# A trunk kernel on one Trainium2 core: six attention heads of layer 1 multiply whole fp32 values in four-pass products, two heads to a PSUM bank

## The chip, the core and the metric

The kernel runs on one core of a Trainium2 chip. The core has five engines that work side by side: PE (TensorE, the matrix engine; its weight loads are shown as PEld), DVE (VectorE), ACT (ScalarE), POOL (GpSimd) and SP (SyncE, which issues the DMAs here). PE writes its results to PSUM, eight banks of 128 rows by 512 fp32 columns; POOL works on SBUF alone in this kernel. The metric is the device time of one execution in microseconds (us); less is better.

## The reference, cut to what matters

Two decoder layers on 512 tokens of width 1024, all in fp32. Layer 0 has a sparse attention of another kind, layer 1 has the "NSA" mixer; each runs beside a small attention over 256 memory rows, and each layer ends in a SwiGLU block. The change concerns layer 1's 12 token heads of 64 columns each, in two groups of six that share keys and values. Head by head, three softmax results are multiplied with three sets of values and summed with gates:

```python
    o_c = jnp.einsum('btgjc,bcgd->btgjd', p_c.astype(v_cmp.dtype), v_cmp)
    ...
    o_s = jnp.einsum('bgtjk,bgtkd->btgjd', p_s, v_sel)
    ...
    o_w = jnp.einsum('btgjk,bkgd->btgjd', p_w, vw_i)
    o = gi[..., 0:1] * o_c + gi[..., 1:2] * o_s + gi[..., 2:3] * o_w
```

`o_c` is the compressed branch (31 compressed keys), `o_s` the selected-block branch and `o_w` the window branch. With 512 tokens both of these see every earlier key.

## The kernel before, in words

Everything is kept transposed, with channels on the partitions and the 512 tokens on the columns. To keep fp32 precision on PE, most operands are split into two fp32r parts, hi (the value rounded to fp32r) and lo (what is left), and a product is made of two or three fp32r matmuls (`mm3`, lines 177 to 179). Where an operand stays plain fp32, one matmul instruction does a full-precision product; the change calls this "four-pass".

Layer 1 is a written-out order of units (`SEQ[1]`, line 51): `q:j` projects the queries of head pair j, `h:n` and `w:n` make the softmax rows of head n for the selected and the window branch (`nsa_first`), `H:n` and `W:n` multiply them with the values (`nsa_second`), `c:j` and `C:j` are the compressed branch of a pair, `m`, `o` and others belong to the memory heads and the output projection. Tile, the framework, turns this order into one fixed queue per engine, by its own simulated times, and adds the semaphores.

A unit `H:n` or `W:n` treats its four key blocks in three groups (`KBS`, line 43), of 512, 128 + 384 and 256 columns. For each group it

- transposes the softmax blocks on PE into a "T" bank (line 418, ten transposes of 128x128 to a unit),
- copies the bank to `uh` on ACT (line 426), rounded to fp32r, and subtracts it from the bank on DVE to give `ul` (line 427),
- multiplies each block with the values (line 441), once for `uh` and once for `ul`. The stationary operand is 128 columns wide: 64 of the hi part of the values beside 64 of their lo part.

So the head's "O" bank holds the products with the hi values on rows 0 to 63 and those with the lo values on rows 64 to 127. The compressed branch adds one more fp32r matmul of 512 columns to each head (line 1041), whose operand `ch` is again a hi part on 64 rows (ACT, line 1025) and a lo part on the other 64 (DVE, line 1026). Then `head_out` folds the two halves: an ACT copy of one half (line 449), a DVE add of the other (line 450), the hi part on ACT (line 150) and the lo part on DVE or POOL (line 452 or 83).

The tables in `PLAN` say which engine does which small step; layer 1 runs on rows 4, 5 and then 6, and its turned blocks all take the `"turn": "V"` of row 5, the path just described. Another path, `"F"` (lines 420 to 423), stands in layer 0: one ACT copy to a plain fp32 tile `uf` and one plain fp32 matmul with the 128-column values.

The "O" tag has two banks, "T" four, "S" and "mm" two each; projections take "mm" and "O" in turn.

Of the kernel before, what the change touches and what calls it, by code (L numbers as in the profile page):

```python
# [18 lines left out]
P = 128  # L19
S = 512  # L20
D = 1024
KC = D // P
NB = S // P
NM = 256
# [5 lines left out]
OUT = -3e38  # L30
DOWN_SPLIT = (6, 5)
HALVED = 2
LAST = ("PPVP", "VVVV")
BUFS = {"xs": 17, "p": 10, "u": 8, "q": 12, "z": 2, "q1": 8, "qi": 4, "cy": 2, "k": 8, "m": 6, "r": 3, "t": 6, "o": 26, "o2": 6, "xg": 8}
RINGS = {"wr": 4, "wh": 3, "wl": 3}
STAY = {F32: 7 * KC + 2 + P + KC * S + S + P + NM + 1024 + 592 + RINGS["wr"] * KC * P, F32R: 4 * NB * P + 6 * P + (RINGS["wh"] + RINGS["wl"]) * KC * P}
BANKS = {"mm": 2, "S": 2, "T": 4, "O": 2}
FIRST = (0, 3)
IQ = False
# [3 lines left out]
KBS = ((0,), (3, 1), (2,))  # L43
# [8 lines left out]
 w:5 W:3 C:2 h:4 c:3 q:5 h:5 H:5 mq:0 c:4 H:4 h:6 W:4 C:3 W:5 H:6 c:5 h:8 h:9 mq:1 h:7 mkv w:6 w:7 H:7 m:0 W:6 W:7 o:5 H:8 C:4 w:9 M:0 o:3  # L52
 o:2 m:1 o:1 h:10 o:0 H:9 o:6 W:9 w:8 w:10 M:1 o:7 o:4 W:8 C:5 h:11 H:10 o:12 o:11 w:11 H:11 W:10 o:13 W:11 o:9 o:14 o:8 o:10 o:15"""]
PLAN = [
    {"w": "V", "whi": "A", "stack": "P", "turn": "VP", "scale": "V", "shi": "A", "hhi": "VA", "hlo": "VP", "rmul": "VV", "radd": "V", "phi": "V", "plo": "V", "sqe": "PP", "irow": "VVPP", "sq": "PV"},
    {"w": "PP", "whi": "A", "stack": "P", "turn": "VFF", "scale": "P", "shi": "A", "hhi": "AA", "hlo": "PP", "rmul": "P", "radd": "PV", "phi": "VAAV", "plo": "PPP", "sqe": "AAP", "irow": "P", "sq": "VPP"},
    {"w": "P", "whi": "A", "stack": "VP", "turn": "V", "scale": "PAVA", "shi": "VVV", "hhi": "A", "hlo": "PV", "rmul": "VPVP", "radd": "PV", "phi": "VVV", "plo": "P", "sqe": "PP", "irow": "VPV", "sq": "VP"},
    {"w": "PPV", "whi": "AA", "stack": "PV", "turn": "F", "scale": "PP", "shi": "V", "hhi": "VVVV", "hlo": "VV", "rmul": "P", "radd": "PPP", "phi": "VVV", "plo": "V", "sqe": "VAPV", "irow": "P", "sq": "P"},
    {"w": "VVP", "whi": "VA", "stack": "PV", "turn": "FF", "scale": "A", "shi": "AVA", "hhi": "AA", "hlo": "PV", "rmul": "VV", "radd": "VPV", "phi": "AVVV", "plo": "VPVP", "sqe": "VA", "irow": "VVVV", "sq": "V"},
    {"w": "P", "whi": "AA", "stack": "P", "turn": "V", "scale": "VV", "shi": "A", "hhi": "A", "hlo": "VPP", "rmul": "PVV", "radd": "PP", "phi": "A", "plo": "PV", "sqe": "PA", "irow": "P", "sq": "VPPV"},  # L60
    {"w": "PPP", "whi": "A", "stack": "P", "turn": "V", "scale": "A", "shi": "V", "hhi": "A", "hlo": "VV", "rmul": "PPP", "radd": "P", "phi": "VV", "plo": "V", "sqe": "AVP", "irow": "PVVV", "sq": "PP"},
]
SWAP = [i ^ 8 if i < 16 else i for i in range(32)]
W0 = ["kk", "qi0", "qi1", "qi2", "qi3", "ckv", "qm0", "qm1"] + [f"q{j}" for j in range(6)]
# [3 lines left out]
def r32(ap):  # L68
    return ap.bitcast(F32)
# [25 lines left out]
class Trunk:  # L95
# [543 lines left out]
    def down_last(self, acts):  # L639

        nc, cs, ws = self.nc, range(KC - HALVED, KC), []
        for c in cs:
# [14 lines left out]
        for h in range(2):  # L657
# [294 lines left out]
    def comp_values(self, hv, cw2):  # L952
        nc = self.nc
        ps = self.ps("S")[:, :P]
        for g in range(2):
            nc.tensor.matmul(ps[:64, g * 64 : (g + 1) * 64], hv[:, g], cw2[:, P:], start=True, stop=True)
        self.vc = vc = self.c([P, 2, 2, P], F32R, name="vcmp")
        nc.gpsimd.memset(r32(vc), 0.0)
        src = ps.rearrange("p (g d) -> p g d", g=2)
        for par in range(2):  # L960
            h = slice(32 * par, 32 * par + 32)
            a, b = slice(0, 64), slice(64, P)
            nc.scalar.activation(vc[h, :, par, a], src[h], AF.Copy, scale=0.5)
            for up in (0, 64):
                hu = slice(32 * par + up, 32 * par + up + 32)
                if up:
                    nc.scalar.copy(vc[hu, :, par, a], r32(vc[h, :, par, a]))
                nc.vector.scalar_tensor_tensor(vc[hu, :, par, b], src[h], 0.5, r32(vc[h, :, par, a]), op0=ALU.mult, op1=ALU.subtract)

    def values(self, col, xs):  # L970

        nc, io = self.nc, self.io
        gates = self.gates
        self.ready.add("values")
        ncol = self.small(NB, "ncol", bufs=1)
        nc.vector.tensor_scalar(ncol, col, -1.0, None, op0=ALU.mult)
        out = [self.ps(t)[:, :292] for t in ("mm", "O", "mm", "O")]
        for u in range(3):
            ks = range(3 * u, min(3 * u + 3, KC))
            wt = self.weight(io["w1v"][:, ks.start * 292 : ks.stop * 292], len(ks) * 292)  # L980
            for b in range(NB):
                for i, k in enumerate(ks):
                    self.mm3(out[b], tuple(t[:, b * P : (b + 1) * P] for t in xs[k]), tuple(t[:, i * 292 : (i + 1) * 292] for t in wt),
                             k == 0, k == KC - 1)
        for b in range(NB):
            src = out[b][:, :256].rearrange("p (a d) -> p a d", a=4)
            v = self.vals[:, :, b]
            s = col[:, b : b + 1]
            nc.scalar.activation(v[:, :, 0:64], src, AF.Copy, scale=s)
            nc.vector.scalar_tensor_tensor(v[:, :, 64:128], src, s, r32(v[:, :, 0:64]), op0=ALU.mult, op1=ALU.subtract)  # L990
            nc.scalar.activation(gates[:, b], out[b][:, 256:292], AF.Exp, scale=ncol[:, b : b + 1])
        nc.vector.tensor_scalar(gates, gates, 1.0, None, op0=ALU.add)

# [25 lines left out]
    def compressed_turned(self, j, p):  # L1019
        nc = self.nc  # L1020
        ps = self.ps("T")
        for b in range(NB):
            nc.tensor.transpose(ps[:64, b * P : (b + 1) * P], p[:, b * 64 : (b + 1) * 64], self.ident)
        c = self.slot("t", "ch", F32R)
        nc.scalar.copy(c[:64], ps[:64])
        nc.vector.tensor_sub(c[64:], ps[:64], r32(c[:64]))
        self.comp[j] = c

    def nsa_units(self, h, q, keys):
        j, e, g = h // 2, h % 2, h // 6  # L1030
        shared = {}

        def first(br):
            return self.nsa_first(h, q[h], keys[br][g], br)

        def second(br, ps_):
            if br == 0:
                shared["o"] = self.ps("O")
            self.nsa_second(h, br, shared["o"], ps_)
            if br == 1:  # L1040
                self.nc.tensor.matmul(shared["o"], self.vc[:, g, e], self.comp[j], start=False, stop=True)
                hs = slice(64 * e, 64 * e + 64)
                self.head_out(shared["o"], slice(0, S), e, self.o[j][0][hs], self.o[j][1][hs])
                self.whole[j] += 1

        return [(lambda: first(0), lambda st: second(0, st)), (lambda: first(1), lambda st: second(1, st))]

    def comp_unit(self, j):
        return lambda: self.compressed(j), lambda st: self.compressed_turned(j, st)
# [17 lines left out]
    def nsa_second(self, h, br, o, ps_):  # L1067
        nc = self.nc
        e, g = h % 2, h // 6
        for kbs in KBS:  # L1070
            at, pieces, spans = 0, [], []
            for kb in kbs:
                pieces += [(at + (b - kb) * P, ps_[b][:, kb * P : (kb + 1) * P]) for b in range(kb, NB)]
                spans.append((kb, slice(at, at + S - kb * P)))
                at += S - kb * P
            parts = self.turned(pieces, at)
            for kb, cs in spans:
                self.weighted(o[:, kb * P :], self.vals[:, 2 * br + g, kb], [t[:, cs] for t in parts], br == 0 and kb == 0, False)

    def run(self):  # L1080
        self.turn, self.flip, self.comp, self.two, self.ready = False, False, {}, {}, set()
# [86 lines left out]
```

## Time and profile before

| | |
|---|---|
| time, median of 3 runs | 1277.14 us (1274.31 to 1278.22) |
| the profiled execution | 1273.98 us |
| its span, first to last instruction | 1272.2 us |
| mean granted PE clock | 0.990 |
| instructions | 17057 |
| PE busy | 1226.5 us (96%) |
| DVE busy | 631.0 us (50%) |
| ACT busy | 546.5 us (43%) |
| POOL busy | 769.0 us (60%) |

The profiled execution is a run of its own, with 1.8 us outside the span. Its busy times are averages over stages: the FFN blocks (about 200 to 640 us and from 890 us on) keep PE full, the two attention stages less so. A PE instruction's recorded duration includes a tail during which the next one already runs, so what a matmul costs is read from the distance between two starts.

### The profile page before, as it was taken

Reading aid. Unit: us, or ns where it says so; the run is one execution under the profiler, and the core shown is the slowest. Engines: PE = TensorE matmul, PEld = TensorE weight load, DVE = VectorE, ACT = ScalarE, POOL = GpSimd, SP = SyncE. Lnnn points to the kernel's source line nnn. Section 1 sums busy time; section 2 is a strip of 40 time slices with the busy share of each in tenths; the row PEclk is TensorE's granted clock in tenths of the full one; section 3 lists DMA queues with packets and bytes.
Section 4 is the critical chain, followed back from the end, with each engine's and each line's share of the span. In section 5 each row is a group of like instructions: output and inputs, shape, how many; then the busy total and the mean of one; then the engine's idle time right before and its main releaser. Section 6 shows DMA issues by size and latency. Waiting matters only on the chain. (4 is left out here: it accounts for less than half of the span.)

```text
span 1272.2 us, 17057 instructions
## 1 busy us (share of the span) xinstructions
PE 1226.5 (96%) x5882; PEld 1016.1 (80%) x5882; DVE 631.0 (50%) x1433; ACT 546.5 (43%) x1059; POOL 769.0 (60%) x1070
## 2 busy tenths in 40 slices
PE   7999889999999999999997899999999999999996
PEld 5888558888888888888886788887888888888886
DVE  7799976632221222233678998996531210111113
ACT  5635886332322222322257677785432322332231
POOL 9988874855543455447276553235977656667573
PEclk9999999999999999999998999999999999999998
DMA  7222002233323332223332001113233233333232
GB/s 272 85 86 80 9 1 92 85 98 99 90 81 102 121 90 97 89 82 121 103 100 66 24 13 45 44 32 111 84 102 95 83 91 116 107 97 92 69 91 67
DMA packets 40262, 108.44 MB, mean 85 GB/s; under 512 B 4720, under 2 KB 10480, under 8 KB 40176
## 3 DMA queue, kind: packets, MB, share of 16 engines
q1 hardware_dynamic: 40176, 107.36, 27.5%
q8 instruction: 46, 0.75, 0.3%
q14 instruction: 40, 0.33, 0.1%
HBM read 105.25 MB, written 2.10 MB: 84 GB/s over the span
## 5 line engine op out<-in xcount | busy, mean ns | idle before, releaser
L83 POOL TENSOR_TENSOR stay<-stay,stay 128x256 fp32r<-128x256 f32 (+1 forms) x601 | 442.3, 765 | 323.3 <-ACT stay L150 181.5
L150 ACT CAST stay<-stay 128x1024 fp32r<-128x1024 f32 (+4 forms) x208 | 189.4, 911 | 511.8 <-PE ps L178 452.0
L177 PE MATMUL ps<-xh,stay 128*128 128x512 f32 x912 | 357.6, 392 | 7.8 <-ACT xh L238 6.2
L179 PE MATMUL ps<-xh,stay 128*128 128x512 f32 x912 | 358.1, 393 | 1.2 <-DVE stay L165 1.1
L178 PE MATMUL ps<-xl,stay 128*128 128x512 f32 x912 | 357.5, 392 | 0.9 <-DVE xl L239 0.9
L177 PEld LDWEIGHTS ps<-xh,stay 128*128 128x128 f32 x912 | 172.6, 189 | 44.2 <-ACT xh L238 6.2
L179 PEld LDWEIGHTS ps<-xh,stay 128*128 128x128 f32 x912 | 172.5, 189 | 37.9 <-DVE stay L165 2.0
L178 PEld LDWEIGHTS ps<-xl,stay 128*128 128x128 f32 x912 | 172.2, 189 | 37.5 <-DVE xl L239 2.1
L178 PE MATMUL ps<-fl,stay 128*128 128x512 f32 (+1 forms) x352 | 134.8, 383 | 0.0
L179 PE MATMUL ps<-fh,stay 128*128 128x512 f32 (+1 forms) x352 | 134.6, 382 | 0.0
L177 PE MATMUL ps<-fh,stay 128*128 128x512 f32 (+1 forms) x352 | 134.6, 382 | 0.0
L609 DVE TENSOR_TENSOR fa<-fa,ps 128x512 f32<-128x512 f32 x44 | 30.2, 687 | 183.5 <-PE ps L179 166.1
L626 DVE TENSOR_TENSOR stay<-stay,ps 128x512 f32<-128x512 f32 x30 | 20.7, 689 | 155.5 <-PE ps L179 155.5
L606 DVE TENSOR_TENSOR fa<-ps,row 128x512 f32<-128x512 f32 x44 | 30.2, 691 | 129.5 <-PE ps L179 116.2
L391 ACT ACTIVATE p<-p,stay 128x384 f32<-128x384 f32 (+3 forms) x144 | 80.3, 559 | 22.9 <-DVE stay L385 21.3
L83 POOL TENSOR_TENSOR fa<-fa,row 128x256 f32<-128x256 f32 x88 | 65.3, 763 | 25.3 <-ACT fa L607 25.2
L178 PEld LDWEIGHTS ps<-fl,stay 128*128 128x128 f32 x352 | 66.1, 188 | 12.9
L179 PEld LDWEIGHTS ps<-fh,stay 128*128 128x128 f32 x352 | 66.1, 188 | 12.9
L177 PEld LDWEIGHTS ps<-fh,stay 128*128 128x128 f32 x352 | 66.1, 188 | 12.9
L427 DVE TENSOR_TENSOR ul<-ps,uh 128x512 fp32r<-128x512 f32 (+1 forms) x103 | 62.1, 619 | 5.4 <-ACT uh L426 4.7
L426 ACT CAST uh<-ps 128x512 fp32r<-128x512 f32 (+1 forms) x103 | 53.3, 533 | 12.5 <-PE ps L418 11.6
L418 PE MATMUL ps<-stay,p 128*128 128x128 f32 x360 | 54.3, 275 | 4.5 <-DVE stay L385 1.6
(273 smaller groups left out, 1981.2 us busy)
## 6 DMA issues: line engine op xcount, KB each, us to landing
stay<-in_wf SPq DMA_DIRECT2D x88, 512.0 KB, 3.6
stay<-in_w SPq DMA_DIRECT2D x26, 512.0 KB, 3.6
stay<-in_wd SPq DMA_DIRECT2D x32, 384.0 KB, 3.1
stay<-in_wd SPq DMA_DIRECT2D x32, 320.0 KB, 2.8
mem<-in_memT SPq DMA_DIRECT2D x12, 256.0 KB, 3.9
stay<-in_wo SPq DMA_DIRECT2D x6, 512.0 KB, 3.6
stay<-in_wo SPq DMA_DIRECT2D x16, 192.0 KB, 2.4
stay<-in_xT SPq DMA_DIRECT2D x8, 256.0 KB, 6.8
```

Source lines behind the costliest of these rows:

```text
L83: op(out[:, sl], x[:, sl], y[:, sl])
L150: self.nc.scalar.copy(out, x)
L177: mm(out, lhs[0], rhs[0], start=start, stop=False)
L178: mm(out, lhs[0], rhs[1], start=False, stop=False)
L179: mm(out, lhs[1], rhs[0], start=False, stop=stop)
L391: self.nc.scalar.activation(p, p, AF.Exp, scale=-1.0, bias=least, accum_out=total)
L418: nc.tensor.transpose(ps[:, off : off + P], ap, self.ident)
L426: nc.scalar.copy(hi, ps[:, :w])
L427: nc.vector.tensor_sub(lo, ps[:, :w], r32(hi))
L606: nc.vector.tensor_mul(a, g, row)
L609: nc.vector.tensor_mul(a, a, u)
L626: nc.vector.tensor_add(self.x[d], self.x[d], ps)
```

## The change

For the heads of group 0 (heads 0 to 5, `WHOLE = (0,)`) the values are no longer split. Heads 6 to 11 stay as they are.

- `values` writes the group's values to a plain fp32 tile with one ACT instruction for each token block, and the split (ACT, then DVE) is made for the other group alone. `comp_values` likewise makes the compressed values of group 0 as one plain tile for the two heads of a pair.
- `whole_second` takes the place of `nsa_second`: the same transposes, one ACT copy of the bank to a plain tile `uf`, and one four-pass matmul for each block with 64 stationary columns, whose result goes to rows 0 to 63 of a bank for the even head and to rows 64 to 127 of the same bank for the odd head. The `ul` subtraction is gone.
- `compressed_turned` keeps a plain copy on 64 rows for these pairs; one four-pass matmul of 512 columns serves both heads of the pair.
- `head_out` is not called for these heads. When both branches of both heads are in the bank, `hi` is copied from it on ACT and `lo` is subtracted from it on DVE, 128 rows at once.

The diff, cut to its core:

```diff
+WHOLE = (0,)
...
 PLAN = [
...
+    {"w": "P", "full": "A", "whi": "A", "stack": "P", "turn": "V", "scale": "VV", "shi": "A", "hhi": "A", "hlo": "VPP", "rmul": "PVV", "radd": "PP", "phi": "A", "plo": "PV", "sqe": "PA", "irow": "P", "sq": "VPPV"},
...
     def comp_values(self, hv, cw2):
...
+            if g in WHOLE:
+                self.vc[g] = vc = self.c([P, P], name="vcmp")
+                nc.gpsimd.memset(vc, 0.0)
+                for par in range(2):
+                    h = slice(32 * par, 32 * par + 32)
+                    nc.scalar.activation(vc[h, 64 * par : 64 * par + 64], src[h], AF.Copy, scale=0.5)
+                continue
...
     def values(self, col, xs):
...
+        self.whole_vals = {g: self.c([P, 2, NB, 64], name="wv") for g in WHOLE}
...
+            for g in range(2):
+                if g in WHOLE:
+                    nc.scalar.activation(self.whole_vals[g][:, :, b], src[:, g::2], AF.Copy, scale=s)
+                    continue
+                v = self.vals[:, g::2, b]
+                nc.scalar.activation(v[:, :, 0:64], src[:, g::2], AF.Copy, scale=s)
+                nc.vector.scalar_tensor_tensor(v[:, :, 64:128], src[:, g::2], s, r32(v[:, :, 0:64]), op0=ALU.mult, op1=ALU.subtract)
...
-        c = self.slot("t", "ch", F32R)
-        nc.scalar.copy(c[:64], ps[:64])
-        nc.vector.tensor_sub(c[64:], ps[:64], r32(c[:64]))
+        if j // 3 in WHOLE:
+            c = self.slot("t", "ch")
+            nc.scalar.copy(c[:64], ps[:64])
...
         def second(br, ps_):
+            if g in WHOLE:
+                return self.whole_second(h, br, ps_)
...
+    def whole_second(self, h, br, ps_):
+        nc = self.nc
+        j, e, g = h // 2, h % 2, h // 6
+        if j not in self.pairs:
+            self.pairs[j] = [self.ps("O"), set()]
+        o, done = self.pairs[j]
+        rows = slice(64 * e, 64 * e + 64)
+        for kbs in KBS:
+            pieces, spans, at = self.gathered(kbs, ps_)
+            ps = self.ps("T")
+            for off, ap in pieces:
+                nc.tensor.transpose(ps[:, off : off + P], ap, self.ident)
+            t = self.slot("u", "uf")[:, :at]
+            self.copy("full", t, ps[:, :at])
+            for kb, cs in spans:
+                nc.tensor.matmul(o[rows, kb * P :], self.whole_vals[g][:, br, kb], t[:, cs], start=kb == 0 and not any(d[0] == e for d in done),
+                                 stop=False, skip_group_check=True)
+        done.add((e, br))
+        if len(done) == 4:
+            nc.tensor.matmul(o, self.vc[g][:64], self.comp[j][:64], start=False, stop=True, skip_group_check=True)
+            hi, lo = self.o[j]
+            self.copy("hhi", hi, o)
+            nc.vector.tensor_sub(lo, o, r32(hi))
+            self.whole[j] += 2
```

`gathered` is the loop of `nsa_second` that collects the blocks of a group, moved to a function of its own.

## Rows read from the trace of the kernel before

**Rows 1.** The page, part 1: busy time, share of the span and instructions of each engine.

```profile
PE 1226.5 (96%) x5882; PEld 1016.1 (80%) x5882; DVE 631.0 (50%) x1433; ACT 546.5 (43%) x1059; POOL 769.0 (60%) x1070
```

**Rows 2.** Busy time of each engine in stretches of layer 1's attention stage: the stretch, its length, then busy us and instructions of PE, PEld, DVE, ACT and POOL, the granted PE clock, DMA share, GB/s.

```profile
660.00:690.00 30.00, 24.58 (x139) 20.86 (x138) 25.90 (x74) 22.62 (x58) 22.17 (x30) 0.89 0.23 71
690.00:776.00 86.00, 79.07 (x483) 67.73 (x482) 84.00 (x248) 61.49 (x157) 41.58 (x56) 1.00 0.07 20
776.00:890.00 114.00, 110.80 (x606) 94.56 (x606) 96.96 (x258) 79.52 (x208) 41.06 (x62) 1.00 0.22 63
```

**Rows 3.** Who PE's matmuls waited for between 690 and 776 us: total us, times, longest us.

```profile
PE ps L441 <- DVE ul L427: 3.7, 4, 1.7
PE ps L418 <- DVE stay L385: 1.6, 2, 1.3
PE ps L380 <- DVE rb L329: 0.7, 1, 0.7
PE ps L177 <- DVE ul L427: 0.7, 1, 0.7
```

**Rows 4.** The same waits seen from PE's weight loads, between 690 and 776 us.

```profile
PEld ps L441 <- DVE ul L427: 5.8, 8, 2.1
PEld ps L418 <- DVE stay L385: 2.1, 2, 1.5
PEld ps L177 <- DVE ul L427: 1.1, 1, 1.1
PEld ps L380 <- DVE rb L329: 0.9, 1, 0.9
PEld ps L380 <- DVE stay L385: 0.7, 2, 0.4
```

**Rows 5.** Groups of DVE's instructions between 690 and 776 us: line, shapes, count, busy us, mean ns of one, idle time before.

```profile
L427 DVE TENSOR_TENSOR ul<-ps,uh 128x512 fp32r<-128x512 f32 x24 | 16.1, 680 | 0.0
L427 DVE TENSOR_TENSOR ul<-ps,uh 128x256 fp32r<-128x256 f32 x12 | 4.9, 406 | 0.1
L450 DVE TENSOR_TENSOR ho<-ho,ps 64x512 f32<-64x512 f32 x6 | 4.0, 674 | 0.1
```

**Rows 6.** Two more of DVE's lines between 690 and 776 us, each from the view of its own line or tile: count, duration in ns (least, median, most), first and last start.

```profile
L452 DVE TENSOR_TENSOR ol<-ho,oh x2: 689/954/1220, 712.0 to 752.2; 64x512 fp32r<-64x512 f32 x2
L1026 DVE TENSOR_TENSOR ch<-ps,ch x4: 684/684/685, 697.4 to 771.5; 64x512 fp32r<-64x512 f32 x4
```

**Rows 7.** Groups of ACT's instructions between 690 and 776 us, as in rows 5.

```profile
L426 ACT CAST uh<-ps 128x512 fp32r<-128x512 f32 x24 | 13.6, 577 | 4.4 <-PE ps L418 4.1
L449 ACT COPY ho<-ps 64x512 f32<-64x512 f32 x6 | 3.5, 581 | 2.6 <-PE ps L1041 2.5
```

**Rows 8.** The timeline of PE's matmuls from 706 us on: start, recorded duration, line, shapes, count, and in brackets the idle time before it and what ended it.

```profile
706.21 0.33 PE L441 MATMUL ps<-ul,stay 128*128 128x128 f32 x1 [1.68 <-DVE ul L427]
706.37 0.39 PE L441 MATMUL ps<-uh,stay 128*128 128x384 f32 x1
706.60 0.34 PE L441 MATMUL ps<-ul,stay 128*128 128x384 f32 x1
706.78 0.28 PE L441 MATMUL ps<-uh,stay 128*128 128x256 f32 x1
706.90 0.27 PE L418 MATMUL ps<-stay,p 128*128 128x128 f32 x1
```

**Rows 9.** The timeline of PE's matmuls in layer 0, where plain fp32 products (`uf`, and `mem` in the second part) stand among fp32r ones.

```profile
128.96 0.39 PE L441 MATMUL ps<-ul,stay 128*128 128x512 f32 x1
129.19 1.02 PE L441 MATMUL ps<-uf,stay 128*128 128x512 f32 x2
129.64 0.80 PE L177 MATMUL ps<-mkh,oh 128*128 128x512 f32 x1
130.28 0.40 PE L178 MATMUL ps<-mkl,oh 128*128 128x512 f32 x1
...
111.51 2.97 PE L489 MATMUL ps<-mem,stay 128*128 128x256 f32 x13
114.32 0.38 PE L505 MATMUL ps<-stay,mem 128*128 128x256 f32 x1
```

**Rows 10.** The timeline of PE's matmuls around four instructions whose stationary operand has 64 columns (128*64).

```profile
693.77 0.28 PE L381 MATMUL ps<-tl,sa 128*128 128x256 f32 x1
693.89 0.60 PE L1023 MATMUL ps<-stay,pc 128*64 128x128 f32 x4
694.33 0.49 PE L418 MATMUL ps<-stay,p 128*128 128x128 f32 x3
```

**Rows 11.** Layer 0's plain copies of a turned bank, from the view of line 422 (count, duration in ns as least, median and most, first and last start), and, from the view of line 441, the idle time that PE and PEld had before that line until such a copy came (us, times).

```profile
L422 ACT COPY uf<-ps x15: 560/585/605, 127.0 to 178.4; 128x512 f32<-128x512 f32 x15
...
  ACT uf L422: 3.1, 5
```

**Rows 12.** The timeline of PE's matmuls, one line of head 0's first unit.

```profile
676.80 0.48 PE L441 MATMUL ps<-ul,stay 128*128 128x128 f32 x1 [0.76 <-DVE ul L427]
```

**Rows 13.** Who PE's weight loads waited for between 776 and 890 us, two of the rows.

```profile
PEld ps L177 <- DVE stay L385: 1.5, 1, 1.5
PEld ps L441 <- DVE ul L427: 1.4, 3, 0.8
```

More of the change, by code (lines that the diff above doesn't have):

```diff
@@ L35 @@
 RINGS = {"wr": 4, "wh": 3, "wl": 3}
-STAY = {F32: 7 * KC + 2 + P + KC * S + S + P + NM + 1024 + 592 + RINGS["wr"] * KC * P, F32R: 4 * NB * P + 6 * P + (RINGS["wh"] + RINGS["wl"]) * KC * P}
+STAY = {F32: 7 * KC + 2 + P + KC * S + S + P + NM + 1024 + 592 + len(WHOLE) * (2 * NB * 64 + P) + RINGS["wr"] * KC * P, F32R: 4 * NB * P + 6 * P + (RINGS["wh"] + RINGS["wl"]) * KC * P}
 BANKS = {"mm": 2, "S": 2, "T": 4, "O": 2}
@@ L54 @@
 PLAN = [
-    {"w": "V", "whi": "A", "stack": "P", "turn": "VP", "scale": "V", "shi": "A", "hhi": "VA", "hlo": "VP", "rmul": "VV", "radd": "V", "phi": "V", "plo": "V", "sqe": "PP", "irow": "VVPP", "sq": "PV"},
-    {"w": "PP", "whi": "A", "stack": "P", "turn": "VFF", "scale": "P", "shi": "A", "hhi": "AA", "hlo": "PP", "rmul": "P", "radd": "PV", "phi": "VAAV", "plo": "PPP", "sqe": "AAP", "irow": "P", "sq": "VPP"},
-    {"w": "P", "whi": "A", "stack": "VP", "turn": "V", "scale": "PAVA", "shi": "VVV", "hhi": "A", "hlo": "PV", "rmul": "VPVP", "radd": "PV", "phi": "VVV", "plo": "P", "sqe": "PP", "irow": "VPV", "sq": "VP"},
@@ L58 @@
-    {"w": "PPV", "whi": "AA", "stack": "PV", "turn": "F", "scale": "PP", "shi": "V", "hhi": "VVVV", "hlo": "VV", "rmul": "P", "radd": "PPP", "phi": "VVV", "plo": "V", "sqe": "VAPV", "irow": "P", "sq": "P"},
-    {"w": "VVP", "whi": "VA", "stack": "PV", "turn": "FF", "scale": "A", "shi": "AVA", "hhi": "AA", "hlo": "PV", "rmul": "VV", "radd": "VPV", "phi": "AVVV", "plo": "VPVP", "sqe": "VA", "irow": "VVVV", "sq": "V"},
-    {"w": "P", "whi": "AA", "stack": "P", "turn": "V", "scale": "VV", "shi": "A", "hhi": "A", "hlo": "VPP", "rmul": "PVV", "radd": "PP", "phi": "A", "plo": "PV", "sqe": "PA", "irow": "P", "sq": "VPPV"},
@@ L61 @@
-    {"w": "PPP", "whi": "A", "stack": "P", "turn": "V", "scale": "A", "shi": "V", "hhi": "A", "hlo": "VV", "rmul": "PPP", "radd": "P", "phi": "VV", "plo": "V", "sqe": "AVP", "irow": "PVVV", "sq": "PP"},
+    {"w": "V", "full": "A", "whi": "A", "stack": "P", "turn": "VP", "scale": "V", "shi": "A", "hhi": "VA", "hlo": "VP", "rmul": "VV", "radd": "V", "phi": "V", "plo": "V", "sqe": "PP", "irow": "VVPP", "sq": "PV"},
+    {"w": "PP", "full": "A", "whi": "A", "stack": "P", "turn": "VFF", "scale": "P", "shi": "A", "hhi": "AA", "hlo": "PP", "rmul": "P", "radd": "PV", "phi": "VAAV", "plo": "PPP", "sqe": "AAP", "irow": "P", "sq": "VPP"},
@@ new lines @@
+    {"w": "P", "full": "A", "whi": "A", "stack": "VP", "turn": "V", "scale": "PAVA", "shi": "VVV", "hhi": "A", "hlo": "PV", "rmul": "VPVP", "radd": "PV", "phi": "VVV", "plo": "P", "sqe": "PP", "irow": "VPV", "sq": "VP"},
+    {"w": "PPV", "full": "A", "whi": "AA", "stack": "PV", "turn": "F", "scale": "PP", "shi": "V", "hhi": "VVVV", "hlo": "VV", "rmul": "P", "radd": "PPP", "phi": "VVV", "plo": "V", "sqe": "VAPV", "irow": "P", "sq": "P"},
+    {"w": "VVP", "full": "A", "whi": "VA", "stack": "PV", "turn": "FF", "scale": "A", "shi": "AVA", "hhi": "AA", "hlo": "PV", "rmul": "VV", "radd": "VPV", "phi": "AVVV", "plo": "VPVP", "sqe": "VA", "irow": "VVVV", "sq": "V"},
@@ L62 @@
+    {"w": "P", "full": "A", "whi": "AA", "stack": "P", "turn": "V", "scale": "VV", "shi": "A", "hhi": "A", "hlo": "VPP", "rmul": "PVV", "radd": "PP", "phi": "A", "plo": "PV", "sqe": "PA", "irow": "P", "sq": "VPPV"},
+    {"w": "PPP", "full": "A", "whi": "A", "stack": "P", "turn": "V", "scale": "A", "shi": "V", "hhi": "A", "hlo": "VV", "rmul": "PPP", "radd": "P", "phi": "VV", "plo": "V", "sqe": "AVP", "irow": "PVVV", "sq": "PP"},
 ]
@@ L956, in comp_values @@
             nc.tensor.matmul(ps[:64, g * 64 : (g + 1) * 64], hv[:, g], cw2[:, P:], start=True, stop=True)
[L957 to L968, printed above, removed]
+        self.vc = {}
+        for g in range(2):
+            src = ps[:, g * 64 : (g + 1) * 64]
+            if g in WHOLE:
[5 more added lines that the diff above has]
+                continue
+            self.vc[g] = vc = self.c([P, 2, P], F32R, name="vcmp")
+            nc.gpsimd.memset(r32(vc), 0.0)
+            for par in range(2):
+                h = slice(32 * par, 32 * par + 32)
+                a, b = slice(0, 64), slice(64, P)
+                nc.scalar.activation(vc[h, par, a], src[h], AF.Copy, scale=0.5)
+                for up in (0, 64):
+                    hu = slice(32 * par + up, 32 * par + up + 32)
+                    if up:
+                        nc.scalar.copy(vc[hu, par, a], r32(vc[h, par, a]))
+                    nc.vector.scalar_tensor_tensor(vc[hu, par, b], src[h], 0.5, r32(vc[h, par, a]), op0=ALU.mult, op1=ALU.subtract)
     def values(self, col, xs):
@@ L986, in values @@
             src = out[b][:, :256].rearrange("p (a d) -> p a d", a=4)
-            v = self.vals[:, :, b]
             s = col[:, b : b + 1]
-            nc.scalar.activation(v[:, :, 0:64], src, AF.Copy, scale=s)
-            nc.vector.scalar_tensor_tensor(v[:, :, 64:128], src, s, r32(v[:, :, 0:64]), op0=ALU.mult, op1=ALU.subtract)
+            for g in range(2):
+                if g in WHOLE:
[4 more added lines that the diff above has]
+                nc.vector.scalar_tensor_tensor(v[:, :, 64:128], src[:, g::2], s, r32(v[:, :, 0:64]), op0=ALU.mult, op1=ALU.subtract)
             nc.scalar.activation(gates[:, b], out[b][:, 256:292], AF.Exp, scale=ncol[:, b : b + 1])
@@ L1023, in compressed_turned @@
             nc.tensor.transpose(ps[:64, b * P : (b + 1) * P], p[:, b * 64 : (b + 1) * 64], self.ident)
-        c = self.slot("t", "ch", F32R)
-        nc.scalar.copy(c[:64], ps[:64])
-        nc.vector.tensor_sub(c[64:], ps[:64], r32(c[:64]))
+        if j // 3 in WHOLE:
+            c = self.slot("t", "ch")
+            nc.scalar.copy(c[:64], ps[:64])
+        else:
+            c = self.slot("t", "ch", F32R)
+            nc.scalar.copy(c[:64], ps[:64])
+            nc.vector.tensor_sub(c[64:], ps[:64], r32(c[:64]))
         self.comp[j] = c
@@ L1040, in second @@
             if br == 1:
-                self.nc.tensor.matmul(shared["o"], self.vc[:, g, e], self.comp[j], start=False, stop=True)
+                self.nc.tensor.matmul(shared["o"], self.vc[g][:, e], self.comp[j], start=False, stop=True)
                 hs = slice(64 * e, 64 * e + 64)
@@ L1070, in nsa_second @@
         for kbs in KBS:
[L1071 to L1075, printed above, removed]
+            pieces, spans, at = self.gathered(kbs, ps_)
             parts = self.turned(pieces, at)
@@ L1078, in nsa_second, with gathered @@
                 self.weighted(o[:, kb * P :], self.vals[:, 2 * br + g, kb], [t[:, cs] for t in parts], br == 0 and kb == 0, False)
+    def gathered(self, kbs, ps_):
+        at, pieces, spans = 0, [], []
+        for kb in kbs:
+            pieces += [(at + (b - kb) * P, ps_[b][:, kb * P : (kb + 1) * P]) for b in range(kb, NB)]
+            spans.append((kb, slice(at, at + S - kb * P)))
+            at += S - kb * P
+        return pieces, spans, at
     def run(self):
+        self.pairs = {}
         self.turn, self.flip, self.comp, self.two, self.ready = False, False, {}, {}, set()
```

## The prediction

> **What bounds the kernel now.** The page first: PE is busy 96% of the span [rows 1], so one would look for a gain in PE's own work. That share is an average. The stretches of layer 1's attention show another stage [rows 2]: from 690 to 776 us, which holds the products of heads 0 to 5 except the first unit of head 0, DVE is busy 84.00 of 86 us while PE shows 79.07. From 776 to 890 us, where heads 6 to 11 run, DVE falls to 96.96 of 114. So in the first stretch DVE is full and PE waits for it; behind it PE is the bound again.
>
> The waits say the same. Between 690 and 776 us all that the matmuls waited for is DVE [rows 3]: 3.7 + 0.7 us for `ul`, 1.6 us for a score read out late (line 385), 0.7 us for a rope step. The weight loads show longer waits for the same things, 5.8 + 1.1 us and 2.1 + 0.9 + 0.7 us [rows 4]. The two views bracket the truth. A 512-column fp32r matmul is recorded with 0.39 us, while the next starts 0.23 us later [rows 9], so each matmul wait is shown about 0.16 us too short, and waits under 0.16 us are not shown. A weight load runs ahead of its matmul, so its wait is shown too long.
>
> **What the change takes from DVE.** The twelve units of heads 0 to 5 have 24 subtractions of 512 columns and 12 of 256, as many as the stretch shows: 24 x 0.680 + 12 x 0.406 = 21.2 us [rows 5]. (The stretch misses head 0's first unit and holds one of head 6.) The six adds of `head_out` go, 6 x 0.674 = 4.0 us [rows 5], two `lo` subtractions, 2 x 0.954 = 1.9 us, and three of `ch`, 3 x 0.684 = 2.1 us [rows 6]. What comes is three `lo` subtractions from PSUM at 128x512, by the same shape's 0.680 us: 2.0 us. Together 27.2 us less, nearly a third of DVE's 84.00 us.
>
> That is off PE's own queue, so only the waits turn into time.
>
> - Waits for `ul`: 4.4 us in five waits [rows 3], with 0.16 us added to each 5.2 us, and a little for four short ones that only the weight loads show [rows 4]. I take 5.5; the bounds are 4.4 and 6.9.
> - Waits for scores and rope, 2.3 us in three waits [rows 3], with the tails 2.8; bounds 0 and 3.7 [rows 4]. These steps stand in DVE's queue behind the subtractions that go, but each also has work of its own ahead of it. I take two thirds, 1.9 us.
> - Head 0's first unit, before the stretch, waited 0.76 us for `ul` [rows 12], with the tail 0.9 us. What is late next after it is its last blocks' copy on ACT, idle a quarter of that stretch [rows 2], so I take all of it.
>
> **What it changes on PE.** The transposes stay. A unit's eight fp32r matmuls become four plain ones. Their step is in layer 0: from the first `uf` product (129.19) to the second fp32r matmul behind the pair (130.28) is 1.09 us, less 0.23 for the fp32r one 0.86, so 0.43 us for each 512 columns; thirteen of 256 columns take 2.81 us, 0.216 each [rows 9]. That is 0.84 ns a column, and 1280 columns of a unit cost 1.08 us. The fp32r unit costs 2 x 0.23 for 512 columns, 0.23 + 0.18 for 384, 0.12 twice for 256 [rows 8, 9], and for the two of 128 columns 0.06 each by columns: 1.23 us. So 0.15 us a unit, 1.8 us in twelve; by columns alone (0.23 / 512) it would be 1.15 us a unit and 0.9 us in all. The three pairs' compressed products change 2 x 0.23 into 0.43, 0.1 us. I take 1.5; the bounds are 0.9 and 1.9.
>
> No row has a plain product of 64 columns that lands on rows 64 to 127. The nearest are the compressed branch's transposes, 128*64 on rows 0 to 63: the first follows the 256-column matmul before it by 0.12 us, its usual step, four of them take 0.44 us, as do the 128*128 ones behind them by their starts (0.11 each), and neither switch shows a gap [rows 10]. I take nothing for switching and 0.84 ns a column for 64 columns too. The upper bound is a drained array at each switch (below).
>
> The Trainium skill speaks against this: "TensorEngine Tiling (Array Packing)", Key Properties, says that a change of tiling mode, though not of the tile, drains the engine. The trace does not agree for its one pair of switches, 0.12 and 0.11 us by the steps in [rows 10]; by the rule the sum would shrink by 72 drains. Its page "FP8 and Floating Point Precision", TensorE Precision Notes, says a true fp32 product takes four passes; if a pass cost what an fp32r matmul costs, 512 columns would be 0.92 us by an estimate, where [rows 9] give 0.43.
>
> **What it adds on ACT.** The copy to `uf` takes the place of the one to `uh`, 0.585 us against 0.577 [rows 7, 11]. Six copies of 0.581 us [rows 7] and six `hi` copies leave for three `hi` copies of 128x512. `values` gains four ACT instructions of half the width. All of it is hidden: ACT has 61.49 us of work in the 86 [rows 2]; without that cover, each would cost its own 0.3 to 0.6 us. But now PE waits for ACT where it waited for DVE. Layer 0's fifteen such copies made PE and its loads wait 3.1 us in all [rows 11], 0.2 us each, which for 36 copies would be 7.4 us. In the stretch itself 36 copies on the same queue caused no wait that [rows 3] list. I take a cost of 1.0 us, near the row from the stage itself.
>
> A pair now holds one "O" bank from its first product to its last copies, where each head held one in turn. A projection or the next pair queues for the other bank. I take nothing: two heads in succession held as long, and overlapping heads held two.
>
> **The sum.** 5.5 + 1.9 + 0.9 + 1.5 - 1.0 = 8.8 us. The profiled execution took 1273.98 us, so one like it takes 1265.2. The median of the runs before, 1277.14, lies 3.16 us above, so I forecast a median of 1268.3 us.
>
> **The rivals.**
>
> - *Everything DVE held up is lifted.* The longest views of the waits count, 6.9 + 3.7 + 0.9, with 1.9 from PE and no wait for ACT: 13.4 us, 1263.7. DVE's head start could also lift the 2.9 us after 776 us [rows 13]: 16.3 us, 1260.8. Against the second: DVE has 17 us of slack there already [rows 2]. I give a gain over 12 us one chance in ten.
> - *The waits come back elsewhere.* The queues are ordered anew. If products wait for ACT as in layer 0, 7.4 us in place of 1.0, 2.4 us remain: 1274.7. For it: ACT shows 4.4 us of waiting for PE's transposes just before these copies [rows 7], so transpose, copy and product form a chain with little ahead of it. Against it: the chain loses 0.68 us of DVE in each group, and PE has scores and projections to put between. 0.16.
> - *Switching drains PE (slower).* Each group goes from 128-column transposes to 64-column products and back: 36 groups, 72 switches. A drained start costs the 0.16 us tail and about 0.10 us for a weight load in the open, as in the step of 0.16 us behind the stall in [rows 8] against 0.06: 0.26 x 72 = 18.7 us, less 8.8, so 9.9 us slower: 1287.0. It eats the gain at 0.12 us a switch and is slower by over 0.3% from 0.18. Against it stand [rows 10], though for rows 0 to 63 alone. 0.08. The rule quoted above is this rival's.
> - *A 64-column plain product costs twice the rows' price*, 1.72 ns a column: 12 x 1.08 + 3 x 0.43 = 14.2 us, less 8.8: 1282.5. Nothing but the missing row speaks for it. 0.04. That the subtractions stay somewhere can't be: the new path has no operand for them.
>
> **How the numbers follow.** The forecast itself has 0.62, with 1264.5 to 1272.5 as its own range (gains of 4.6 to 12.6 us, some terms at their bounds, not all at once). The faster cases end near 1260, the returned waits near 1275, the doubled product at 1282.5; leaving out the drain, most of the doubled product and the very end of the fast tail loses under 2 in 10, so 1260 to 1281. A change under 0.3% (3.8 us) can't be told from none here. Faster by more: nearly all of 0.62, the 0.10 and a little of 0.16, 0.72. Same: 0.16. Slower: 0.12.
>
> **What would show it.** Right: in the stretch of heads 0 to 5 DVE drops from 98% busy to about three quarters, the waits for `ul` are gone there, and the stretch is 8 to 9 us shorter with as much PE work; two 512-column products are 0.43 us apart; the stretch after 776 us keeps its length. Wrong: PE waits for line 426's successor on ACT by several us, starts of products after transposes slip by more than 0.1 us, or DVE stays full because its later work moved up and PE still waits for scores.

## The result

The changed kernel takes 1283.62 us (median of 4 runs, 1283.49 to 1283.90), against 1275.92 us for the kernel before in the same comparison: a ratio of 1.0054, 95% interval 1.0039 to 1.0068. It is slower by 0.54%, above the range of the forecast (1260 to 1281 us), where a gain was expected. The profiled execution took 1283.9 us with a span of 1282.1.

The page's first part, of the changed kernel:

```profile
PE 1244.9 (97%) x5882; PEld 1010.7 (79%) x5882; DVE 608.8 (47%) x1389; ACT 540.8 (42%) x1056; POOL 761.4 (59%) x1063
```

DVE is busy 22 us less (the forecast of 27.2 us added up single durations, which overlap in the busy time), but PE is busy 18 us more, with exactly as many instructions as before (5882, [rows 1]). A change that was to halve a unit's matmuls should have had fewer. The stretches of layer 1's attention (the columns are those of [rows 2]):

```profile
660.00:690.00 30.00, 26.48 (x141) 20.53 (x140) 22.68 (x67) 22.47 (x59) 21.95 (x30) 0.89 0.22 71
690.00:776.00 86.00, 86.00 (x435) 56.73 (x434) 61.65 (x202) 53.46 (x140) 37.66 (x52) 1.00 0.07 19
776.00:790.00 14.00, 14.00 (x69) 9.79 (x68) 9.94 (x41) 9.26 (x28) 0.62 (x1) 1.00 0.08 26
790.00:903.00 113.00, 109.91 (x598) 93.26 (x597) 91.56 (x230) 77.07 (x194) 40.34 (x61) 1.00 0.21 65
```

From 690 to 776 us DVE falls from 84.00 to 61.65 us and PE is busy for every one of the 86 us; the view of PE's waits in that stretch, which had four rows before [rows 3], is empty. Yet it gets 435 matmuls done there where it did 483. The products of heads 0 to 5 now end near 782 us, and what follows comes about ten microseconds later (the last matmul on the memory rows, line 489 before and 490 now, starts at 802.7 us in place of 792.2). So the waits were lifted as forecast, and PE's own work grew by more than they were worth. Where it grew stands in the view of the new products' line, and in the timeline of PE around some of them:

```profile
L1084 PE MATMUL ps<-uf,stay x96: 272/486/1116, 674.9 to 781.6; 128*64 128x512 f32 x24, 128*64 128x128 f32 x24, 128*64 128x384 f32 x24, 128*64 128x256 f32 x24
```

```profile
720.17 0.39 PE L179 MATMUL ps<-xl,stay 128*128 128x512 f32 x1
720.39 0.39 PE L180 MATMUL ps<-xh,stay 128*128 128x512 f32 x1
720.71 1.07 PE L1084 MATMUL ps<-uf,stay 128*64 128x512 f32 x2
721.72 0.50 PE L178 MATMUL ps<-xh,stay 128*128 128x512 f32 x1
722.05 0.39 PE L179 MATMUL ps<-xl,stay 128*128 128x512 f32 x1
722.28 0.39 PE L180 MATMUL ps<-xh,stay 128*128 128x512 f32 x1
```

Two things are to be seen. First, twelve units have 12 products of 512 columns, and the line shows 24: a plain fp32 product, one matmul call in the kernel, is two recorded instructions. One 512-column product stands as "x2" at 720.71. Second, the steps around it are long. The matmul at 720.39 is followed after 0.32 us, where its kind steps by 0.23; from 720.71 to 721.72 it is 1.01 us, where two instructions of 0.43 make 0.86; and the first fp32r matmul behind takes 0.33 in place of 0.23. That is 0.09 + 0.15 + 0.10 = 0.34 us for going to 64 columns and back. The queue has 33 such blocks of narrow products (some of the 36 groups stand directly behind one another). In the 31 of them that start after 690 us the same differences add up to 9.9 us, 0.32 us each: about 0.30 where a transpose follows, about 0.35 where a 512-column matmul does.

### The profile page after: what moved, and what is told of

Read it like the earlier page. It is cut to its first block, busy times and chain, and to the rows that moved or that the text cites. A ratio compares the mean times of both kernels' runs of the same rounds, so it can differ in the third digit from the quotient of the medians.

```text
span 1282.1 us, 16988 instructions
## 1 busy us (share of the span) xinstructions
PE 1244.9 (97%) x5882; PEld 1010.7 (79%) x5882; DVE 608.8 (47%) x1389; ACT 540.8 (42%) x1056; POOL 761.4 (59%) x1063
## 4 chain that ended last, share of the span: by engine, by line
PE 79%; DVE 12%; POOL 3%; ACT 3%; issue 1%; DMA 0%; SPq 0%; DVEq 0%; ACTq 0%; POOLq 0%
PE ps L180 22%; PE ps L179 22%; PE ps L178 22%; PE ps L1084 3%; POOL sq L84 2%; PE ps L442 2%; DVE sc L691 2%; DVE stay L690 2%; PE ps L419 1%; PE ps L381 1%; PE ps L1080 1%; PE ps L382 1%; DVE p L386 1%; DVE ul L428 1%; POOL stay L84 1%
## 5 line engine op out<-in xcount | busy, mean ns | idle before, releaser
L166 DVE TENSOR_TENSOR stay<-stay,stay 128x1024 fp32r<-128x1024 f32 (+4 forms) x38 | 45.0, 1185 | 27.6 <-ACT stay L151 26.9
L386 DVE CUSTOM_DVE_ANT_0 p<-ps,stay 128x128 f32<-128x128 f32 (+1 forms) x108 | 46.0, 459 | 16.2 <-PE ps L382 13.4
L613 DVE TENSOR_TENSOR fl<-fa,fh 128x512 fp32r<-128x512 f32 x44 | 36.1, 822 | 24.3 <-ACT fh L612 24.3
```

Source lines behind the costliest of these rows:

```text
L166: self.engine("w").tensor_sub(lo, raw, r32(hi))
L386: nc.vector.tensor_tensor_reduce(out=p[:, sl], in0=ps[:, sl], in1=bias, op0=ALU.add, op1=ALU.min, scale=-0.125, scalar=3e38, accum_out=lea ...
L613: nc.vector.tensor_sub(lo, a, r32(hi))
```

## The experiments

All times are medians with the ratio to the kernel before on the same chip, and its 95% interval. The framework orders the queues anew for each version, so a difference of two versions can hold a change of order as well; the run on the order alone, below, shows 5 us from that.

**The products widened to 128 columns.** The values stand beside 64 columns of zeros, so no product is narrow and the other head's rows get zeros added.

```diff
-        self.whole_vals = {g: self.c([P, 2, NB, 64], name="wv") for g in WHOLE}
+        self.whole_vals = {g: self.c([P, 2, NB, 192], name="wv") for g in WHOLE}
...
-                nc.tensor.matmul(o[rows, kb * P :], self.whole_vals[g][:, br, kb], t[:, cs], start=kb == 0 and not any(d[0] == e for d in done),
+                nc.tensor.matmul(o[:, kb * P :], self.whole_vals[g][:, br, kb, 64 - 64 * e : 192 - 64 * e], t[:, cs], start=kb == 0 and not done,
```

> The changed kernel with its products widened: 128 stationary columns, the values beside 64 columns of zeros, so that the other head's rows get zeros added and no product uses a 64-column array. Passes, copies and DVE's work stay as in the changed kernel. Theory (switching): the changed kernel's trace shows a group's first 64-column product 0.09 us late, its second start 0.05 us late, the next 128-column instruction 0.09 us late and the one behind that 0.11 us late, 0.34 us a group, so 36 groups cost about 12 us: 1271 to 1274 here against 1283.6. Rival (passes and a new order alone): the switches are hidden or belong to the waits, and it stays at 1281 to 1284.

Measured: 1275.57 us, 0.9993 (0.9982 to 1.0004), that is 8 us under the changed kernel with the same passes; the theory had 10 to 13. Its timeline:

```profile
701.83 0.33 PE L382 MATMUL ps<-tl,sb 128*128 128x384 f32 x1
702.00 1.02 PE L1085 MATMUL ps<-uf,stay 128*128 128x512 f32 x2
702.86 0.60 PE L1081 MATMUL ps<-stay,p 128*128 128x128 f32 x4
```

The product starts a usual 0.17 us after a 384-column matmul and takes 0.86 us to the next instruction: no extra step on either side. So the extra steps belong to the 64-column width. They add up to about 10 us in the changed kernel's trace, and without them the kernel is 8 us faster.

**DVE's relief alone.** The kernel before, without the lo part of heads 0 to 5's turned blocks: the second product of each block reads a tile of zeros.

```diff
...
+        if drop:
+            nc.scalar.copy(hi, ps[:, :w])
+            lo = self.nolo[:, :w]
...
```

> The kernel before, with the lo part of heads 0 to 5's turned blocks left out: the second fp32r product of each block multiplies a constant tile of zeros, so DVE's 36 subtractions go and PE does just what it did. It prices DVE's relief by itself. By the terms of the prediction (5.5 + 1.9 + 0.9 us of waits) it is 7 to 9 us faster than before, 1267 to 1269. If the changed kernel's loss is the sum of 14 us of doubled passes and 12 us of switches, the relief must be worth about 18 us, and this run would come to 1257 to 1262. If DVE was never what PE waited for, 1274 to 1277.

Measured: 1270.17 us, 0.9952 (0.9936 to 0.9968), 7.3 us faster. PE's waits between 690 and 776 us, where [rows 3] had 6.7 us, are

```profile
PE ps L445 <- ACT uh L427: 0.9, 1, 0.9
PE ps L418 <- DVE stay L385: 0.8, 1, 0.8
PE ps L493 <- DVE stay L385: 0.6, 1, 0.6
```

The prediction's terms for the waits, 8.3 us, are at the upper end of what this interval allows (4.1 to 8.2 us), with 6 of the 27 us that were to go from DVE still there: they hold nearly. The high price of relief that the loss seemed to need (18 us) does not.

**Plain products of 128 columns.** The kernel before, with heads 0 to 5 on layer 0's path F.

```diff
...
-        if e == "F":
+        if e == "F" or whole:
...
```

> The kernel before, with the turned blocks of heads 0 to 5 kept plain and multiplied with the old 128-column values in plain fp32 products (layer 0's path F): the subtractions go, head_out and the compressed branch stay, and no 64-column product is there. Theory (passes): each product is two instructions at 0.84 ns a column, 2.15 us a unit against 1.23, so 11 us more PE time than e3_no_ul. The time is that of e3_no_ul plus 9 to 11 us. Rival (a plain product costs 0.43 us for 512 columns in all, as the prediction had it): no more than e3_no_ul.

Measured: 1277.53 us, 1.0003 (0.9993 to 1.0014), 7.4 us over the run before it, where 9 to 11 were expected. Three of a unit's four products, without a pause:

```profile
702.27 1.89 PE L441 MATMUL ps<-uf,stay 128*128 128x512 f32 x6
703.99 0.27 PE L418 MATMUL ps<-stay,p 128*128 128x128 f32 x1
```

Products of 512, 128 and 384 columns are six instructions and take 1.72 us: 1.68 ns a column, twice the prediction's 0.84. The doubled products use up all that DVE's relief gives. Why the step is only 7.4 us was not tested. PE's 11 us more may fill pauses that the run with zeros still has, and the mean granted clock of this run's executions was higher, 0.987 against 0.984, which goes with about 1 us (estimated from the last section's figures).

**One pass.** The changed kernel with bf16 values and blocks.

```diff
-        self.whole_vals = {g: self.c([P, 2, NB, 64], name="wv") for g in WHOLE}
+        self.whole_vals = {g: self.c([P, 2, NB, 64], BF, name="wv") for g in WHOLE}
...
-            t = self.slot("u", "uf")[:, :at]
+            t = self.slot("u", "uf").bitcast(BF)[:, :at]
```

> The changed kernel with the values and turned blocks of heads 0 to 5 written as bf16, so that their products are one pass (the lower bits of both are left out). Stationary width, switches, copies and DVE's work stay. Theory (passes and switches are both paid): the products cost about 0.23 us for 512 columns in place of 0.86, 1.5 us less a unit, 18 us for twelve; PE is then no longer full in that stretch, so not all of it shows: 1265 to 1270, and a switch still leaves its gaps in the trace. Rival (the loss is all switching or order): 1280 or over.

Measured: 1273.88 us, 0.9970 (0.9959 to 0.9981). It gains 10 us on the changed kernel, less than expected, though more than the rival allowed. The switches are there with one instruction of another type, too: 0.32 us from the matmul before it, then 0.33 to the next and 0.33 to the one after that, where 512 columns step by 0.23:

```profile
722.05 0.39 PE L181 MATMUL ps<-xh,stay 128*128 128x512 f32 x1
722.37 0.40 PE L1085 MATMUL ps<-uf,stay 128*64 128x512 bf16 x1
722.70 0.50 PE L179 MATMUL ps<-xh,stay 128*128 128x512 f32 x1
723.03 0.40 PE L180 MATMUL ps<-xl,stay 128*128 128x512 f32 x1
```

In the stretch ahead, PE's granted clock was low for longer in the profiled execution:

```profile
660.00:690.00 30.00, 27.27 (x126) 22.79 (x125) 23.14 (x62) 20.68 (x54) 23.24 (x31) 0.67 0.23 71
```

0.67 against 0.89 in the kernel before and in the changed kernel: some 20 of the 30 us at 1.2 GHz in place of about 7. Over all executions the mean granted clock was 0.983 here and 0.988 in the changed kernel, which goes with about 2 us of the missing time (an estimate, from the last section's figures). What else is missing was not settled.

**A pair's products side by side.** Since the two heads write different rows, their products might run at once. The even head's are held back and issued in turn with the odd head's, group by group.

```diff
...
+            for kb, cs in spans:
+                for rows, t in made:
+                    nc.tensor.matmul(o[rows, kb * P :], self.whole_vals[g][:, br, kb], t[:, cs], start=kb == 0 and not done,
+                                     stop=False, skip_group_check=True)
...
```

> The changed kernel with the even head's products held back until the odd head's are ready, and then issued in turn, rows 0 to 63 and rows 64 to 127, block by block. Passes stay; groups that switch fall from 36 to 18. If the two column halves of the array work at the same time, a pair's two products take the time of one: 13 us of products and 6 us of switches less, about 1265. If they run one after the other, only the switches halve: 1276 to 1278. If holding the even head back costs more than that, 1280 or over.

Measured: 1290.39 us, 1.0103 (1.0084 to 1.0122), the slowest of all. The halves do overlap where their products meet:

```profile
699.45 1.56 PE L1091 MATMUL ps<-uf,stay 128*64 128x512 f32 x4 [0.24 <-ACT uf L151]
```

Four 512-column instructions in 1.56 us, tail included, are under four steps of 0.43. But the fixed queue that the framework made sets most products apart again: it has 32 blocks of narrow products, where the changed kernel has 33, so the switches stay and little is shared. And where the changed kernel runs head 0's products (674.9 to 680.6 us), PE now stands still and waits for DVE:

```profile
678.01 0.69 PE L957 MATMUL ps<-stay 128*64 128x64 f32 x4 [3.91 <-DVE stay L894]
688.74 0.50 PE L178 MATMUL ps<-xh,stay 128*128 128x512 f32 x1 [3.30 <-DVE stay L386]
```

These two waits are as long as the loss, but the pair blocks below have nearly the same two (3.90 and 3.25 us), so how the loss divides stays open.

**Pair blocks.** All transposes and copies of both heads first, then the eight products queued behind the last transpose, the last copied block first, so that they stand in the queue as one block.

```diff
...
+        with self.tc.issue_after(last.ins if hasattr(last, "ins") else last):
+            for rows, kb, t in reversed(jobs):
+                nc.tensor.matmul(o[rows, kb * P :], self.whole_vals[g][:, br, kb], t, start=kb == 0 and not done, stop=False, skip_group_check=True)
...
```

> The changed kernel with a pair's two heads held together: all transposes and copies of both heads' same branch first, then their eight products in one block, even and odd head in turn, one pair of switches to a block (6 blocks in place of 36 groups). Passes by instruction stay. In the run with the products side by side, two products on different halves started 0.009 us apart and ran together. Theory: a block of 16 instructions takes little over half its serial 4.3 us, 2.4 us, so 11 us of products and 10 us of switches less than the changed kernel; holding the even head back costs part of it, as in that run (7 us): 1268 to 1276. Rival (holding back costs more than the products): 1284 or over.

Measured: 1274.95 us, 0.9977 (0.9967 to 0.9986): 9 us under the changed kernel and 0.2% under the kernel before. Its queue has the six blocks that were asked for.

**Pair blocks in an order of their own.** In `SEQ[1]` the steps of heads 0 to 5 go by pairs (`H:0 H:1`, `W:0 W:1`) in place of a head at a time, so that a pair's blocks are made one behind the other.

```diff
-       """plan:4 vc ks kc q:0 v ck kw h:0 plan:5 cv q:1 c:0 w:0 c:1 H:0 h:1 C:0 W:0 w:1 q:2 h:2 w:2 H:1 C:1 W:1 q:3 H:2 h:3 w:3 q:4 c:2 H:3 w:4 W:2
- w:5 W:3 C:2 h:4 c:3 q:5 h:5 H:5 mq:0 c:4 H:4 h:6 W:4 C:3 W:5 H:6 c:5 h:8
+       """plan:4 vc ks kc q:0 v ck kw h:0 plan:5 cv q:1 c:0 h:1 w:0 C:0 H:0 H:1 w:1 q:2 c:1 h:2 W:0 W:1 C:1 h:3 q:3 w:2 H:2 H:3 w:3 q:4 c:2 h:4 W:2 W:3
+ C:2 h:5 c:3 q:5 w:4 H:4 H:5 mq:0 w:5 c:4 h:6 C:3 W:4 W:5 H:6 c:5 h:8
...
```

> As the pair blocks, with the written order of units changed so that the two heads of a pair are scored one behind the other and neither waits long for its partner. If holding back was a cost, this is 3 to 7 us faster than the pair blocks in the old order, 1263 to 1270, and faster than the kernel before. If not, the same time.

Measured: 1270.63 us, 0.9948 (0.9935 to 0.9961); a second time 1270.94, 0.9950:

> The pair blocks in their own order for heads 0 to 5, a second time beside the run with both groups: 1269 to 1273, and 0.4 to 0.65% under the kernel before.

Both kernels are beaten. A block on its timeline:

```profile
709.06 0.40 PE L381 MATMUL ps<-th,sa 128*128 128x512 f32 x1
709.39 2.37 PE L1092 MATMUL ps<-uf,stay 128*64 128x512 f32 x16
711.69 0.69 PE L1095 MATMUL ps<-ch,stay 64*128 64x512 f32 x1
```

Sixteen instructions, the products of two units, take 2.30 us from 709.39 to 711.69. One after the other they would take 2 x 1280 x 1.68 ns = 4.3 us, and two units of the kernel before took 2.5. The two halves run at the same time from one end of the block to the other, at one pair of switches for a block.

**That order alone**, with the changed kernel's separate products: only the lines of `SEQ[1]` above are changed.

> The changed kernel, products one by one as it has them, in the written order of units that the faster pair blocks used. If the order is what made the pair blocks faster, it gains as they did from their old to their new order (4 us) or more: 1275 to 1280. If pairing is what pays, 1282 to 1287.

Measured: 1289.01 us, 1.0091 (1.0077 to 1.0106). That is above both ranges. The order by itself costs 5 us; under it, pairing is worth 18.

**Pair blocks for both groups.** `WHOLE = (0, 1)`, and the order of heads 6 to 11 likewise in pairs.

```diff
-WHOLE = (0,)
+WHOLE = (0, 1)
...
-        self.vals = self.c([P, 4, NB, P], F32R, name="vals")
+        self.vals = self.c([P, 1, NB, P], F32R, name="vals")
...
+ C:2 h:5 c:3 q:5 w:4 H:4 H:5 mq:0 w:5 c:4 h:6 C:3 W:4 W:5 h:7 c:5 mq:1 w:6 H:6 H:7 w:7 mkv h:8 W:6 W:7 m:0 h:9 o:5 C:4 w:8 H:8 H:9 w:9 M:0 o:3
+ o:2 m:1 o:1 h:10 W:8 W:9 o:0 o:6 h:11 M:1 o:7 o:4 C:5 w:10 H:10 H:11 o:12 w:11 o:11 o:13 o:9 o:14 W:10 W:11 o:8 o:10 o:15"""]
```

> The pair blocks in their own order, for heads 6 to 11 too (the values of both groups plain, twelve blocks of eight products). Theory: what a pair block saves (DVE's subtractions, at PE time that two halves share) it saves again, though PE is already fuller behind 776 us, where only some 3 us of waits for DVE stand: 2 to 5 us under the run with one group, 1265 to 1269. If the last pairs, which have little other work beside them, pay for being held back, 1270 to 1274.

Measured: 1266.79 us, 0.9920 (0.9900 to 0.9940), beside the second run of one group: 4 us more. DVE from 776 to 890 us:

```profile
776.00:890.00 114.00, 113.58 (x616) 88.30 (x615) 78.99 (x206) 72.62 (x191) 38.13 (x56) 1.00 0.20 61
```

78.99 us of DVE in place of 96.96 [rows 2]. This is the fastest version run here.

**A third of the subtractions on POOL.** The kernel before with `turn` as `VVP` in row 5 of `PLAN`, where it was `V`.

```diff
-    {"w": "P", "whi": "AA", "stack": "P", "turn": "V", "scale": "VV", "shi": "A", "hhi": "A", "hlo": "VPP", "rmul": "PVV", "radd": "PP", "phi": "A", "plo": "PV", "sqe": "PA", "irow": "P", "sq": "VPPV"},
+    {"w": "P", "whi": "AA", "stack": "P", "turn": "VVP", "scale": "VV", "shi": "A", "hhi": "A", "hlo": "VPP", "rmul": "PVV", "radd": "PP", "phi": "A", "plo": "PV", "sqe": "PA", "irow": "P", "sq": "VPPV"},
```

> The kernel before with every third turned block of layer 1 taking the existing path over POOL: a plain copy and the hi part on ACT, the subtraction on POOL. It relieves DVE of 24 subtractions with no word of PE's work changed. By the price of DVE's relief (7.3 us for 36 subtractions in the stretch where DVE is full) 2 to 4 us faster than before, if ACT and POOL hide their 0.6 and 1.5 us each; if a block waits for POOL, the same or slower.

Measured: 1283.36 us, 1.0048 (1.0035 to 1.0062), slower. DVE is relieved by little in the stretch, and PE works no more than before:

```profile
690.00:776.00 86.00, 79.15 (x467) 67.72 (x465) 80.87 (x235) 62.16 (x164) 48.21 (x65) 0.98 0.06 19
```

From 690 us on, PE's loads wait 4.1 us for the copies on ACT (lines 426 and 434) and 0.9 us for POOL's `ul`, and still 3.8 us for DVE's. In this profile too the stretch before 690 us ran at a granted clock of 0.67. But the timed executions had the same mean granted clock as the kernel before beside them (0.982 and 0.983), so the clock does not explain the loss; the longer way of the turned blocks is left, by argument and not by a test.

## Why the prediction was wrong

- **What bounds the stage: right.** DVE was full and PE waited for it. With the subtractions gone, the waits in the stretch are gone, DVE is at 61.65 of 86 us (72%; three quarters were forecast), and the relief of the subtractions alone is worth 7.3 us, where the three wait terms sum to 8.3.
- **The price of a product: wrong, by a factor of two.** The step was "0.43 us for each 512 columns", read from two `uf` entries and thirteen `mem` entries of [rows 9]. Those are instructions, not products, and a plain product is two of them. The evidence stood in the trace of the kernel before: [rows 11] have 15 copies, each read by one product (path F, one block to a copy), and line 441 has 30 `uf` instructions. Likewise `mem_kv` calls line 489 16 times a layer, 32 in all, and the trace counts 64:

```profile
L441 PE MATMUL ps<-uf,stay x20: 590/592/674, 129.2 to 182.6; 128*128 128x512 f32 x20
L441 PE MATMUL ps<-uf,mv x10: 590/592/844, 141.3 to 156.5; 128*128 128x512 f32 x10
L489 PE MATMUL ps<-mem,stay x64: 377/379/430, 100.6 to 792.2; 128*128 128x256 f32 x64
```

So the term was not a gain of 1.5 us but a loss: by 1.68 ns a column, 12 x (2.15 - 1.23) = 11.0 us for the units; the pairs' compressed products take 1.05 us each by their steps (781.95 to 783.00 for the last), 3 x (1.05 - 0.46) = 1.8 us. On the clock the units' products cost 7.4 us (plain products of 128 columns against the run with zeros).

- **The rule on four passes, dismissed too soon.** The Trainium skill, "FP8 and Floating Point Precision", TensorE Precision Notes, gives a true fp32 product four passes. The estimate by that, 0.92 us for 512 columns, is near the 0.86 measured. The row that was set against it counted half a product, and the rival of the double price, which is the same claim, was priced at 0.04 without it.
- **Switching: taken as nothing, 0.32 us a block.** [Rows 10] were the nearest rows, but these are transposes. Between 128-column matmuls the 64-column width costs nothing there, and 0.30 to 0.35 us in a product, for the even and the odd heads alike. Widening the products took back 8 us. The changed kernel's trace shows more of the transposes:

```profile
771.43 0.65 PE L1084 MATMUL ps<-uf,stay 128*64 128x256 f32 x2
772.01 0.63 PE L1038 MATMUL ps<-stay,pc 128*64 128x128 f32 x4
772.57 1.07 PE L1084 MATMUL ps<-uf,stay 128*64 128x512 f32 x2
```

Here the same four transposes stand between narrow products. They take 0.56 us to the next start, where [rows 10] have 0.44, and the two 256-column instructions ahead take 0.58, where twice 0.216 make 0.43. So a step between a narrow product and a narrow transpose costs about what one to a wide transpose does: the width alone does not decide, and [rows 10] held no switch of the kind that the change adds. Why is open. The Trainium skill's rule, "TensorEngine Tiling (Array Packing)", Key Properties, that a change of tiling mode drains the engine, agrees with the products, and with the transposes if they count as wide.

- **The rivals.** The two slow ones, 0.08 for the drain and 0.04 for the double price, both came true, the drain at about 0.16 us a switch in place of 0.26. Each was set against the full gain; that both could hold at once had no chance and no time. That the double price's 1282.5 lies near the measured 1283.62 is luck: on the clock that price cost 7.4 us and the 1.5 that were not gained, 8.9 where its sum had 14.2, and the switches, which it left out, made up the rest. By the medians of the runs, 7.3 us of relief less 7.4 for the doubled products and 8.0 for the switches, plus 2.0 for the rest, is a loss of 6.1 us; the result's own comparison gives 7.7 (5.0 to 8.7 by its interval). The rest (the merged `head_out`, the compressed products, the wait for ACT) was not priced piece by piece: it is the step from the plain 128-column products to the widened ones, about what the intervals leave.
- **ACT.** No wait of PE's matmuls for ACT's `uf` is listed in the stretch, and its weight loads show 0.8 us. That term, 1.0 us, was too high if anything, which decided nothing.

## What to carry to other kernels

Count a row's instructions against the calls in the code before taking its mean as the price of a call: here one plain fp32 product is two entries, which the 30 entries behind 15 copies showed beforehand and the total of 5882 confirmed. Work taken off the engine that delays PE is worth its waits, some 7 us for 21 us of subtractions, and is spent at once if PE pays for it. Here narrow products were worth their switches only in blocks with both halves of the array at work.

## What was not expected of the hardware

- Two products on the two halves of the array run at the same time: sixteen instructions in 2.30 us, half of their serial time. Here it shows only where the queue has them next to each other. The Trainium skill states such overlap in "TensorEngine Tiling (Array Packing)", Key Properties, and the trace agrees.
- A change of width between products and other matmuls costs 0.09 us going in, 0.05 us at the product's second entry and 0.15 to 0.20 us coming out (spread over two steps). With bf16, which has one entry to a product, it is 0.09 going in and 0.20 coming out. A 64-column transpose among 128-column matmuls costs nothing (steps of 0.12 and 0.11 us, [rows 10]), and next to a narrow product it is one more change.
- PE's granted clock differed between the profiled executions ahead of the products: from 660 to 690 us it was 0.89 before and after the change, 0.77 in the run with zeros and 0.67 with bf16 and with POOL's third. It differs between executions of one kernel as well: 0.77 and 0.83 in the two profiles of the pair blocks in their own order. Among the 66 executions of the kernel before that were timed beside the experiments, the six with a mean granted clock of 0.990 took 1273.7 to 1274.8 us, and the twenty with 0.979 or 0.980 took 1277.8 to 1281.0: some 0.4 us for each 0.001. So a difference of a few microseconds between single executions can go with the clock alone, and medians still carry a part of it.
